# Hybrid attention and state-space block on one core: when the attention's sums, the gates' products and the gated unit's tanh are issued

## The chip, the core and the metric

The kernel runs on one core of a Trainium2 chip. The time is device microseconds of one execution. The kernel before took 1146.03 us in the median of three runs (1145.88 to 1149.12). The engines are TensorE (PE: matmuls; PEld: its weight loads), VectorE (DVE), ScalarE (ACT), GpSimd (POOL) and SyncE (SP, which issues most transfers). Each engine works through its own queue in the order in which the program issues; an instruction that waits holds up everything behind it on its engine.

## The reference

One decoder block on 512 tokens and 16 meta tokens, 1024 wide: a half-weighted SwiGLU unit, then a mixer, then a second half-weighted SwiGLU unit, with a norm ahead of each and one at the end. The mixer runs sliding-window attention and a state-space layer side by side and merges them through two sigmoid gates:

```
hn = rmsnorm(h, mix_norm)
q, k, v, u, g_attn, g_ssm = split(hn @ w_in)
attn = sliding_window_attention(q, k, v, sinks)     # 16 heads, 4 key heads, window 128, 16 meta keys, one sink per head
y = gelu(s5_ssm(u))
ssm = (y @ glu_a) * sigmoid(y @ glu_b)
merged = sigmoid(g_attn) * attn + sigmoid(g_ssm) * ssm
h = h + merged @ w_out
```

Everything is float32. The kernel keeps that precision by splitting each operand of a product into a high and a low part (`hi`, `lo`) and summing three matmuls (hi·hi, hi·lo, lo·hi) for one.

## The kernel before

**Units.** The work of TensorE is a row of units. A unit holds 128 output rows: its weights arrive by SyncE's transfers as raw float32, are split ahead of time by `prep_piece` (ScalarE copies the high part, line 173; VectorE subtracts to get the low part `wlo`, line 174), and are then used by 24 matmuls of 512 columns (line 238). Other work that TensorE must do is issued between these matmuls: `accumulate` (line 223) takes a list of callbacks and calls them at even distances. In the mixer that list has eleven places, cut 0 to cut 10.

**The mixer's thirty units** (loop from line 1304) are, by `MIX`, two each of: queries q1 (units 0, 1), state gates gs0 (2, 3), gated units glu0 (4, 5), q2 (6, 7), attention gates ga0 (8, 9), gs1 (10, 11), glu1 (12, 13), q3 (14, 15), ga1 (16, 17), gs2 (18, 19), glu2 (20, 21), ga2 (22, 23), gs3 (24, 25), ga3 (26, 27) and glu3 (28, 29). A unit's evacuation is put off into the next unit: `flush` at cut 0 of the next.

**The attention's sixteen blocks** (4 key heads times 4 blocks of 128 queries) run inside these units. Block n begins in unit `BEGIN[n]` and takes three units:

- in the first, `s1` for four heads at cuts 2, 4, 7 and 7: two score matmuls (1167, 1168) into one of two score buffers in PSUM, a masking reduction on VectorE (1170) that frees the score buffer, the exponential on ScalarE (1172); after the fourth head the denominator: `es` (1175, 1176), `den` (1177, 1178), and the probabilities normalised on VectorE (`pm`, the meta keys, 1181) and GpSimd (`E`, 1183);
- in the second, `s2o` and `s2p` at cut 7 transpose the probabilities (1191) and split them into `ph` and `pl` (1194, 1195); `s2m` at cut 8 does it for the meta keys (`ms`, 1212 and 1213), and GpSimd spreads them into `m4` (1215; the profile's name is m);
- in the third, `s3` at cut 5 multiplies by the values (1226) into `pv`, `s3m` at cut 7 adds the meta keys' product (1234), and `s3e` at cut 9 brings the sum out. The values are stored as high and low halves side by side, so `pv` has two halves of 64 partitions, and the sum of the two is the attention's output: ScalarE copies the lower half to `tb` (1240), and VectorE adds the halves into `AT` in two instructions (1242).

The PSUM pool of `pv` has one buffer (line 1078), that of the scores two (1076). `tb`, `ta`, `tg` and `tq` share a tag with four buffers (line 1091).

**The gates.** `ev_ga` multiplies an attention gate's output by the norm's factor (1257), takes the tanh (1258), multiplies into `AT` (1259) and, for rows below 6, adds the state-space part (`merge`, 1250). `unit_glu` makes two products of half the depth, `b` and then `a`, each with its own PSUM tile; its evacuation takes the tanh of `b` (1283), multiplies by `a` (1284) and by the state gate (1285). The weights for a later unit are prepared at cut 8. The order within a cut is that in which the loop's body calls `at_cut`.

Of the kernel before, what the change touches and what calls it, by code (L numbers as in the profile page):

```python
# [10 lines left out]
AF = mybir.ActivationFunctionType  # L11
ALU = mybir.AluOpType
# [25 lines left out]
PREPS = (6, 34)  # L38
KS1 = 8
VS = (1, 0, 2, 10, 13, 13)  # L40
CUT = {"s3": 5, "s3m": 7, "s3e": 9, "s1": (2, 4, 7, 7), "s2o": 7, "s2p": 7, "s2m": 8, "prep": 8, "ev": 0, "ks": 10, "vs": 7}
BEGIN = (1, 2, 3, 4, 6, 7, 10, 11, 13, 14, 15, 18, 19, 20, 21, 24)

NG = 32
# [21 lines left out]
def hybrid_block_kernel(  # L66
# [30 lines left out]
    V, S, G, PE, SY = nc.vector, nc.scalar, nc.gpsimd, nc.tensor, nc.sync  # L97
# [13 lines left out]
    def real(t):  # L111
        return t.rearrange("p (h c) -> p h c", h=2)[:, :, :256]
# [118 lines left out]
    def mm3(outs, hi, lo, rhi, rlo, nk, mids, k0=0):  # L231
        seq = []
        for k in range(nk):
            seq += [(hi, rhi, k), (hi, rlo, k), (lo, rhi, k)]

        def emit(w, r, k, start, stop):
            for o, sl in outs:
                PE.matmul(out=o, lhsT=w[:, k0 + k, :], rhs=sl(r, k), start=start, stop=stop)  # L238

        accumulate(seq, emit, mids)  # L240
# [10 lines left out]
    def mm512(ps, hi, lo, rhi, rlo, nk, mids, k0=0, packed=True):  # L251
        if packed:
            mm3([(ps, lambda r, k: r[:, k, :])], hi, lo, rhi, rlo, nk, mids, k0)
        else:
            mm3([(ps, lambda r, k: real(r[:, k, :]))], hi, lo, rhi, rlo, nk, mids, k0)
# [575 lines left out]
    def norm_hook(t_p, h, hgn, n, cols=COLS):  # L831
        def hook(d):
            split_hg(hgn, h, n, d, 0, cols)
            t = t_p.tile([128, cols], F32, tag="t1", name="sqd")
            S.activation(out=t, in_=h[:, d, :], func=AF.Square)
            if d == 0:
                G.tensor_copy(sqs[:, :cols], t)
            else:
                G.tensor_tensor(out=sqs[:, :cols], in0=sqs[:, :cols], in1=t, op=ALU.add)
        return hook  # L840
# [5 lines left out]
    units, _ = ffn_units(hg, hT, True, mm_ps, g_p, t_p, CHUNKS1, norm_hook(t_p, hT, hg2, 1), first_mm)  # L846
# [181 lines left out]
    def h2(t):  # L1028
        return t.rearrange("p (h c) -> p h c", h=2)
# [55 lines left out]
    AT = a_p.tile([128, ND, SEQ], F32, name="AT")  # L1085
# [4 lines left out]
    def tmp(name):  # L1090
        return a_p.tile([128, 512], F32, tag="t", name=name, bufs=4)
# [62 lines left out]

    att = {}

    def s1(n, h):
        k, b = divmod(n, 4)
        W = 144 if b == 0 else 272
        c0 = (0, 0, 144, 272)[b]  # L1160
        if h == 0:
            att[n] = [a_p.tile([128, 4, 272], F32, tag="E", name="E", bufs=2)]
            att[n] += [a_p.tile([128, 4], F32, tag=t, name=t, bufs=2) for t in ("mn", "den", "es")]
        E, mn, den, es = att[n][:4]
        q = Q[2 * k + h // 2][:, h % 2, 128 * b:128 * b + 128]
        ps = sc_ps.tile([128, 512], F32, tag="sc", name="ps_s")
        PE.matmul(out=ps[:, 0:W], lhsT=q, rhs=KH[:, k, c0:c0 + W], start=True, stop=False)  # L1167
        PE.matmul(out=ps[:, 0:W], lhsT=q, rhs=KL[:, k, c0:c0 + W], start=False, stop=True)  # L1168
        mk = mC[:, 128:272] if b == 0 else (mC if b == 2 else mA)
        V.tensor_tensor_reduce(out=E[:, h, 0:W], in0=ps[:, 0:W], in1=mk, scale=1.0,  # L1170
                               scalar=sinkn[:, 4 * k + h:4 * k + h + 1], op0=ALU.add, op1=ALU.min, accum_out=mn[:, h:h + 1])
        S.activation(out=E[:, h, 0:W], in_=E[:, h, 0:W], func=AF.Exp, scale=-1.0, bias=mn[:, h:h + 1], accum_out=den[:, h:h + 1])  # L1172
        if h != 3:
            return
        V.tensor_tensor(out=es, in0=mn, in1=sinkn[:, 4 * k:4 * k + 4], op=ALU.subtract)
        S.activation(out=es, in_=es, func=AF.Exp)
        V.tensor_tensor(out=den, in0=den, in1=es, op=ALU.add)
        V.reciprocal(out=den, in_=den)
        m0 = 128 if b == 2 else 0
        pm = a_p.tile([128, 4, 16], F32, tag="pm", name="pm", bufs=2)  # L1180
        V.tensor_tensor(out=pm, in0=E[:, :, m0:m0 + 16], in1=den.unsqueeze(2).to_broadcast([128, 4, 16]), op=ALU.mult)
        for c, w in (((0, 128), (144, 128)) if b == 2 else ((16, W - 16),)):
            G.tensor_tensor(out=E[:, :, c:c + w], in0=E[:, :, c:c + w], in1=den.unsqueeze(2).to_broadcast([128, 4, w]), op=ALU.mult)
        att[n] = (E, pm, [])
# [45 lines left out]
    pvs = {}  # L1230

    def s3m(n):
        pv, ms = pvs[n]
        PE.matmul(out=pv, lhsT=VM[:, n // 4, :], rhs=ms.rearrange("p h c -> p (h c)"), start=False, stop=True)

    def s3e(n):
        k, b = divmod(n, 4)
        pv, _ = pvs.pop(n)
        tb = tmp("tb")
        S.activation(out=tb[0:64], in_=pv[64:128, :], func=AF.Copy)  # L1240
        for e in range(2):
            V.tensor_tensor(  # L1242
                out=AT[64 * e:64 * e + 64, 2 * k:2 * k + 2, 128 * b:128 * b + 128],
                in0=pv[0:64].rearrange("p (i e c) -> p e i c", e=2, c=128)[:, e],
                in1=tb[0:64].rearrange("p (i e c) -> p e i c", e=2, c=128)[:, e], op=ALU.add)
# [3 lines left out]
    def merge(m):  # L1249
        V.scalar_tensor_tensor(out=AT[:, m, :], in0=gst.pop(m), scalar=0.5, in1=AT[:, m, :], op0=ALU.mult, op1=ALU.add)  # L1250
        if m >= 6:
            msplit(m)

    def ev_ga(m):
        def f(p):
            t = tmp("ta")
            V.tensor_tensor(out=h2(t), in0=p, in1=r512, op=ALU.mult)
            S.activation(out=t, in_=t, func=AF.Tanh, scale=0.5)
            V.scalar_tensor_tensor(out=AT[:, m, :], in0=t, scalar=1.0, in1=AT[:, m, :], op0=ALU.add, op1=ALU.mult)
            if m < 6:  # L1260
                merge(m)
        return f

    def ev_gs(m):
# [7 lines left out]
    def unit_glu(m):  # L1272
        cell = {}

        def mm(hi, lo, mids):
            n = (len(mids) + 1) // 2
            for key, k0, ms in (("b", 4, mids[:n]), ("a", 0, mids[n:])):
                cell[key] = mm_ps.tile([128, 512], F32, tag="mm", name="p")
                mm512(cell[key], hi, lo, YH, YL, 4, ms, k0)

        def ev():
            t = tmp("tg")
            S.activation(out=t, in_=cell["b"], func=AF.Tanh, scale=0.5)
            V.scalar_tensor_tensor(out=t, in0=t, scalar=1.0, in1=cell["a"], op0=ALU.add, op1=ALU.mult)
            V.scalar_tensor_tensor(out=gst[m], in0=gst[m], scalar=1.0, in1=t, op0=ALU.add, op1=ALU.mult)
            if m >= 6:
                merge(m)
        return mm, ev
# [3 lines left out]
    def msplit(m):  # L1292
        S.activation(out=mg[0][:, m, :], in_=AT[:, m, :], func=AF.Copy)
        V.tensor_tensor(out=mg[1][:, m, :], in0=AT[:, m, :], in1=fr(mg[0][:, m, :]), op=ALU.subtract)
# [8 lines left out]
    begin = dict(zip(BEGIN, range(16)))  # L1303
    for i, u in enumerate(units):
        cuts = [[] for _ in range(NCUT)]

        def at_cut(c, f, *a):
            cuts[c].append(lambda: f(*a))

        if i - 2 in begin:  # L1310
            for f, c in ((s3, "s3"), (s3m, "s3m"), (s3e, "s3e")):
                at_cut(CUT[c], f, begin[i - 2])
        if i in begin:
            for h in range(4):
                at_cut(CUT["s1"][h], s1, begin[i], h)
        if i - 1 in begin:
            for f, c in ((s2o, "s2o"), (s2p, "s2p"), (s2m, "s2m")):
                at_cut(CUT[c], f, begin[i - 1])
        at_cut(CUT["ev"], flush)
        if i == KS1:  # L1320
            at_cut(CUT["ks"], ksplit, 1)
            at_cut(CUT["ks"], vmeta, 1)
        for v, iv in enumerate(VS):
            if i == iv:
                at_cut(CUT["vs"], vsplit, *divmod(v, 3))
        at_cut(CUT["prep"], prep_piece)
        if i == len(units) - 2:
            mg += new_hg(SEQ)
            for m in range(6):
                at_cut(m, msplit, m)  # L1330

        step(*u, mids=[lambda fs=fs: [f() for f in fs] for fs in cuts], prep=False, hold=i < len(units) - 1)
# [59 lines left out]
    n = CHUNKS2[-1]  # L1392
# [60 lines left out]
    for j in range(2 * ND):  # L1453
        h, d = divmod(j, ND)
# [48 lines left out]
```

## Time and profile before

| what | value |
|---|---|
| median of three runs | 1146.03 us |
| the profiled execution, its own time | 1148.62 us |
| its span, first to last instruction | 1146.8 us |
| TensorE busy | 1127.8 us, 98% of the span |
| VectorE, ScalarE, GpSimd busy | 636.5, 410.4, 357.1 us |
| the mixer's thirty units | about 498 to 728 us of the span |
| mean granted TensorE clock | 0.990 |

Times in the rows are microseconds from the span's start, then the duration, the engine, the line, the operation, what it writes and reads with its shapes, how many were merged into the row, and in brackets the engine's idle time ahead of it and what ended it. A row of a group gives busy time and the mean of one in ns, a row of waits the engine and line that waited, for whom, the microseconds in total, how often, and the longest. A row of a stretch gives, for each engine, its busy time and its number of instructions, then the granted clock, the share of the transfer engines and GB/s.

### The profile page before, as it was taken

The page shows a single profiled execution, that of the slowest core. Times are in us where ns is not written, and L with a number is a line of the kernel's source. Part 1 is how long each engine was busy: PE and PEld are TensorE (multiplying, and loading weights), DVE is VectorE, ACT ScalarE, POOL GpSimd, SP SyncE. Part 2 cuts the span into 40 slices and gives each one's busy share as a digit, 9 for nine tenths or more (in the row PEclk, how much of TensorE's full clock was granted, in tenths as well). Part 3 has the DMA queues.
Part 4 walks back from the last instruction along what each step waited for, and adds up shares of the span by engine and source line. Part 5 has one row for each costly group of instructions (what it writes and reads, how often), then busy time and mean ns, then how long its engine had stood idle before and what let it go on. Part 6 is the DMA issues. An engine that isn't in the chain of part 4 may idle for free.

```text
span 1146.8 us, 17241 instructions
## 1 busy us (share of the span) xinstructions
PE 1127.8 (98%) x7006; PEld 1006.2 (88%) x7006; DVE 636.5 (55%) x960; ACT 410.4 (36%) x727; POOL 357.1 (31%) x488
## 2 busy tenths in 40 slices
PE   9999999999999999999999999999999999999997
PEld 7999999999999999977778778888888888888887
DVE  5446663655444464867767776664544444444454
ACT  5322232232222242465646554443322321322234
POOL 1966663542883030444444231020000000000003
PEclk7999999999999999999999999999999999999999
DMA  5423233232423246212211222432423224313222
GB/s 164 115 94 110 74 94 112 75 85 84 112 87 95 77 160 170 56 63 74 74 58 53 74 74 81 144 106 74 129 92 111 74 83 127 111 65 128 75 74 74
DMA packets 105583, 108.43 MB, mean 95 GB/s; under 512 B 7504, under 2 KB 101968, under 8 KB 105376
## 3 DMA queue, kind: packets, MB, share of 16 engines
q1 hardware_dynamic: 103104, 100.74, 28.0%
q0 software_dynamic: 2352, 6.52, 2.2%
q8 instruction: 55, 0.90, 0.3%
q14 instruction: 24, 0.20, 0.1%
q10 hardware_dynamic: 48, 0.07, 0.0%
HBM read 100.80 MB, written 5.34 MB: 93 GB/s over the span
## 4 chain that ended last, share of the span: by engine, by line
PE 88%; DVE 5%; ACT 4%; issue 2%; DMA 1%; POOL 0%; SPq 0%; DVEq 0%; POOLq 0%; ACTq 0%
PE p L238 59%; PE p L412 11%; PE p L414 9%; PE p L800 2%; PE pv L1226 1%; PE p L1398 1%; DVE wlo L174 1%; ACT whi L173 1%; PE ps_t L1191 1%; DVE AT L1242 1%; PE ps_s L1167 1%; ACT E L1172 1%; PE ps_s L1168 1%; DMA xb<-in_x_dram 1%; ACT qs L1144 0%
## 5 line engine op out<-in xcount | busy, mean ns | idle before, releaser
L238 PE MATMUL p<-hgh,whi 128*128 128x264 f32 (+1 forms) x1408 | 403.6, 333 | 0.1
L238 PE MATMUL p<-hgl,whi 128*128 128x264 f32 (+1 forms) x1408 | 403.1, 332 | 0.0
L238 PE MATMUL p<-hgh,wlo 128*128 128x264 f32 (+1 forms) x1408 | 401.2, 331 | 0.0
L174 DVE TENSOR_TENSOR wlo<-raw,whi 128x1024 fp32r<-128x1024 f32 (+2 forms) x192 | 257.7, 1342 | 91.6 <-ACT whi L173 89.4
L238 PEld LDWEIGHTS p<-hgh,whi 128*128 128x128 f32 x1408 | 238.9, 188 | 26.0 <-issue 0.8
L238 PEld LDWEIGHTS p<-hgh,wlo 128*128 128x128 f32 x1408 | 238.6, 189 | 23.5
L238 PEld LDWEIGHTS p<-hgl,whi 128*128 128x128 f32 x1408 | 238.9, 188 | 22.4
L173 ACT ACTIVATE whi<-raw 128x1024 fp32r<-128x1024 f32 (+2 forms) x192 | 187.5, 979 | 133.5 <-PE p L414 72.2
L1414 POOL TENSOR_TENSOR acc<-acc,zq 128x256 f32<-128x256 f32 x12 | 8.9, 738 | 349.8 <-ACT zq L1407 349.7
L432 DVE SCALAR_TENSOR_TENSOR hT<-p,hT 128x528 f32<-128x528 f32 (+1 forms) x56 | 39.1, 698 | 87.1 <-PE p L414 52.2
L384 ACT ACTIVATE t<-t 128x528 f32<-128x528 f32 (+1 forms) x44 | 28.1, 639 | 165.0 <-DVE t L383 164.9
L394 ACT ACTIVATE gh<-t 128x528 fp32r<-128x528 f32 (+1 forms) x44 | 28.1, 639 | 160.6 <-DVE t L393 160.6
L412 PE MATMUL p<-gh,whi 128*128 128x264 f32 x352 | 72.6, 288 | 0.7 <-DVE hT L432 0.5
L412 PE MATMUL p<-gl,whi 128*128 128x264 f32 x352 | 71.5, 284 | 0.0
L412 PE MATMUL p<-gh,wlo 128*128 128x264 f32 x352 | 71.4, 284 | 0.0
L383 DVE TENSOR_TENSOR t<-p,r_bc 128x528 f32<-128x528 f32 (+1 forms) x44 | 30.7, 698 | 71.3 <-PE p L238 68.1
L393 DVE TENSOR_TENSOR t<-p,t 128x528 f32<-128x528 f32 (+1 forms) x44 | 30.7, 698 | 65.4 <-PE p L238 65.0
L412 PEld LDWEIGHTS p<-gh,whi 128*128 128x128 f32 x352 | 54.5, 189 | 1.9 <-issue 0.8
L414 PE MATMUL p<-gh,whi 128*128 128x512 f32 x144 | 56.0, 389 | 0.0
L414 PE MATMUL p<-gl,whi 128*128 128x512 f32 x144 | 56.0, 389 | 0.0
L414 PE MATMUL p<-gh,wlo 128*128 128x512 f32 x144 | 56.0, 389 | 0.0
L385 DVE TENSOR_TENSOR t<-t,r_bc 128x528 f32<-128x528 f32 (+1 forms) x44 | 37.2, 846 | 32.4 <-ACT t L384 32.4
(322 smaller groups left out, 1502.2 us busy)
## 6 DMA issues: line engine op xcount, KB each, us to landing
raw<-in_ffn_w_dram SPq DMA_DIRECT2D x42, 1024.0 KB, 5.4
raw<-in_ffn_w_dram SPq DMA_DIRECT2D x24, 768.0 KB, 4.3
raw<-in_w_in_dram SPq DMA_DIRECT2D x16, 1024.0 KB, 5.5
raw<-in_ffn_w_dram SPq DMA_DIRECT2D x12, 512.0 KB, 3.6
raw<-in_w_out_dram SPq DMA_DIRECT2D x4, 1024.0 KB, 8.1
h_keep<-hT POOLq DMA_DIRECT2D x1, 2112.0 KB, 7.3
raw<-in_ssm_glu_a_dram SPq DMA_DIRECT2D x4, 512.0 KB, 3.6
raw<-in_ssm_glu_b_dram SPq DMA_DIRECT2D x4, 512.0 KB, 5.3
```

What stands on the lines that cost most here:

```text
L173: S.activation(out=hi, in_=src, func=AF.Copy)
L174: V.tensor_tensor(out=lo, in0=src, in1=fr(hi), op=ALU.subtract)
L238: PE.matmul(out=o, lhsT=w[:, k0 + k, :], rhs=sl(r, k), start=start, stop=stop)
L383: V.tensor_tensor(out=t1, in0=cell[1], in1=rb(), op=ALU.mult)
L384: S.activation(out=t1, in_=t1, func=AF.Silu)
L385: V.tensor_tensor(out=t1, in0=t1, in1=rb(), op=ALU.mult)
L393: V.tensor_tensor(out=t3, in0=cell[3], in1=cell["t1"], op=ALU.mult)
L394: S.activation(out=gh, in_=t3, func=AF.Copy)
L412: PE.matmul(out=p[:, h, :HALF], lhsT=wt[:, k, :], rhs=gs[k][c][:, h, :], start=start, stop=stop)
L414: PE.matmul(out=p, lhsT=wt[:, k, :], rhs=gs[k][c].rearrange("p h c -> p (h c)"), start=start, stop=stop)
L432: V.scalar_tensor_tensor(out=hv(hT, d), in0=cell["p"], scalar=0.5, in1=hv(hT, d), op0=ALU.mult, op1=ALU.add)
L800: PE.matmul(out=p[:, h, :HALF], lhsT=w[:, k, :], rhs=r[:, k, h * HALF:(h + 1) * HALF], start=(n == 0), stop=(n == 3 * ND - 1))
```

## The change

Three things move; no instruction is added or taken away.

1. `tb` is now issued by `s3m`, right behind the meta keys' product at cut 7, and no longer by `s3e`. The two additions of `s3e` move from cut 9 to cut 7 in units where no new block begins. In the seven units in which the third unit of one block is the first of another (3, 4, 6, 13, 15, 20, 21) they are issued inside that other block's `s1`, after `es` and ahead of `den` (the call `fill`).
2. The second half of an attention gate's evacuation (1259 and the merge) is put into a list of its own, which is emptied at cut 6 of the same unit; the first half stays at cut 0.
3. The tanh of `b` in `unit_glu` is issued right behind `b`'s matmuls, ahead of those of `a`, in the unit itself.

```diff
-CUT = {"s3": 5, "s3m": 7, "s3e": 9, "s1": (2, 4, 7, 7), ..., "prep": 8, "ev": 0, "ks": 10, "vs": 7}
+CUT = {"s3": 5, "s3m": 7, "s3e": 7, "ev2": 6, "s1": (2, 4, 7, 7), ..., "prep": 8, "ev": 0, "ks": 10, "vs": 7}
...
-    def s1(n, h):
+    def s1(n, h, fill):
...
         S.activation(out=es, in_=es, func=AF.Exp)
+        if fill:
+            fill()
         V.tensor_tensor(out=den, in0=den, in1=es, op=ALU.add)
...
     def s3m(n):
         pv, ms = pvs[n]
         PE.matmul(out=pv, lhsT=VM[:, n // 4, :], rhs=ms.rearrange("p h c -> p (h c)"), start=False, stop=True)
+        tb = tmp("tb")
+        S.activation(out=tb[0:64], in_=pv[64:128, :], func=AF.Copy)
+        pvs[n] = (pv, tb)
 
     def s3e(n):
         k, b = divmod(n, 4)
-        pv, _ = pvs.pop(n)
-        tb = tmp("tb")
-        S.activation(out=tb[0:64], in_=pv[64:128, :], func=AF.Copy)
+        pv, tb = pvs.pop(n)
...
+    pend2 = []
+
+    def flush2():
+        while pend2:
+            pend2.pop(0)()
+
     def ev_ga(m):
         def f(p):
             t = tmp("ta")
             V.tensor_tensor(out=h2(t), in0=p, in1=r512, op=ALU.mult)
             S.activation(out=t, in_=t, func=AF.Tanh, scale=0.5)
-            V.scalar_tensor_tensor(out=AT[:, m, :], in0=t, scalar=1.0, in1=AT[:, m, :], op0=ALU.add, op1=ALU.mult)
-            if m < 6:
-                merge(m)
+
+            def second():
+                V.scalar_tensor_tensor(out=AT[:, m, :], in0=t, scalar=1.0, in1=AT[:, m, :], op0=ALU.add, op1=ALU.mult)
+                if m < 6:
+                    merge(m)
+            pend2.append(second)
         return f
...
                 mm512(cell[key], hi, lo, YH, YL, 4, ms, k0)
+                if key == "b":
+                    t = cell["t"] = tmp("tg")
+                    S.activation(out=t, in_=cell["b"], func=AF.Tanh, scale=0.5)
 
         def ev():
-            t = tmp("tg")
-            S.activation(out=t, in_=cell["b"], func=AF.Tanh, scale=0.5)
+            t = cell["t"]
...
-            for f, c in ((s3, "s3"), (s3m, "s3m"), (s3e, "s3e")):
-                at_cut(CUT[c], f, begin[i - 2])
+            at_cut(CUT["s3"], s3, begin[i - 2])
+            at_cut(CUT["s3m"], s3m, begin[i - 2])
+            fill = lambda n=begin[i - 2]: s3e(n)
+            if i not in begin:
+                at_cut(CUT["s3e"], fill)
+        else:
+            fill = None
         if i in begin:
             for h in range(4):
-                at_cut(CUT["s1"][h], s1, begin[i], h)
+                at_cut(CUT["s1"][h], s1, begin[i], h, fill)
...
         at_cut(CUT["ev"], flush)
+        at_cut(CUT["ev2"], flush2)
```

More of the change, by code (lines that the diff above doesn't have):

```diff
@@ L40 @@
 VS = (1, 0, 2, 10, 13, 13)
-CUT = {"s3": 5, "s3m": 7, "s3e": 9, "s1": (2, 4, 7, 7), "s2o": 7, "s2p": 7, "s2m": 8, "prep": 8, "ev": 0, "ks": 10, "vs": 7}
+CUT = {"s3": 5, "s3m": 7, "s3e": 7, "ev2": 6, "s1": (2, 4, 7, 7), "s2o": 7, "s2p": 7, "s2m": 8, "prep": 8, "ev": 0, "ks": 10, "vs": 7}
 BEGIN = (1, 2, 3, 4, 6, 7, 10, 11, 13, 14, 15, 18, 19, 20, 21, 24)
```

## The prediction

> **What bounds the kernel now.** I read the page first, then the stretch in which the changed code runs, then TensorE's waits in that stretch, and last the queues of VectorE, ScalarE and GpSimd around each wait.
>
> ```profile
> span 1146.8 us, 17241 instructions
> PE 1127.8 (98%) x7006; PEld 1006.2 (88%) x7006; DVE 636.5 (55%) x960; ACT 410.4 (36%) x727; POOL 357.1 (31%) x488
> PE 88%; DVE 5%; ACT 4%; issue 2%; DMA 1%; POOL 0%; SPq 0%; DVEq 0%; POOLq 0%; ACTq 0%
> ...
> 498.00:735.00 237.00, 228.30 (x1098) 184.74 (x1096) 172.31 (x377) 130.28 (x302) 88.24 (x59) 0.99 0.24 75
> 735.00:838.00 103.00, 103.00 (x460) 85.44 (x460) 51.60 (x63) 36.93 (x49) 12.07 (x9) 1.00 0.32 102
> ```
>
> TensorE is the bound: busy for 98% of the span and 88% of the chain. It has idle time where the mixer's thirty units run (498 to 735 us, columns PE, PEld, DVE, ACT, POOL): 237.00 − 228.30 = 8.7 us, while the next 103 us have none. So the change is worth at most those waits and what hangs on them. TensorE's waits between 496 and 735 us:
>
> ```profile
> PE ps_s L1167 <- DVE mn L1170: 4.5, 4, 2.0
> PE pv L1226 <- DVE AT L1242: 4.1, 8, 0.9
> ```
>
> ```profile
> 671.46 0.39 PE L238 MATMUL p<-YH,wlo 128*128 128x512 f32 x1
> 671.69 0.40 PE L238 MATMUL p<-YH,whi 128*128 128x512 f32 x1
> 671.93 0.39 PE L1234 MATMUL pv<-m,VM 128*128 128x512 f32 x1
> ...
> 670.00 0.47 PE L1226 MATMUL pv<-ph,VB 128*128 128x512 f32 x1 [0.78 <-DVE AT L1242]
> ...
> 687.11 0.47 PE L1226 MATMUL pv<-ph,VB 128*128 128x512 f32 x1 [0.18 <-DVE AT L1242]
> ```
>
> A matmul's record lasts 0.39 us, but undisturbed starts are 0.23 us apart (671.69 − 671.46). So a wait costs its idle time plus 0.39 − 0.23 = 0.16 us of lost overlap. The eight pv waits cost 4.1 + 8 × 0.16 = **5.4 us**. The pool for pv has one buffer, so the next block's value products cannot start before the sum of L1242 has read the last one.
>
> **Part 1: the sum (s3m, s3e).** Unit 20, a unit whose softmax will take the sum in, shows why it comes late; ScalarE's, TensorE's and GpSimd's rows stand with VectorE's:
>
> ```profile
> 664.74 0.16 DVE L1175 TENSOR_TENSOR es<-mn,sinkn 128x4 f32<-128x4 f32 x1
> 665.56 0.16 DVE L1177 TENSOR_TENSOR den<-den,es 128x4 f32<-128x4 f32 x1 [0.67 <-ACT es L1176]
> ...
> 666.12 0.68 DVE L1195 TENSOR_TENSOR pl<-ps_t,ph 128x512 fp32r<-128x512 f32 x1
> 666.83 0.28 DVE L1213 TENSOR_TENSOR ms<-ps_tm,ms 64x128 fp32r<-64x128 f32 x1
> 667.16 1.93 DVE L174 TENSOR_TENSOR wlo<-raw,whi 128x1024 fp32r<-128x1024 f32 x1
> 669.01 0.84 DVE L1242 TENSOR_TENSOR AT<-pv,tb 64x256 f32<-64x256 f32 x2
> ...
> 663.09 0.39 PE L1234 MATMUL pv<-m,VM 128*128 128x512 f32 x1
> ...
> 664.32 0.52 ACT L1172 ACTIVATE E<-E,mn 128x272 f32<-128x272 f32 x1 [1.95 <-DVE mn L1170]
> ...
> 667.15 0.60 ACT L1240 ACTIVATE tb<-pv 64x512 f32<-64x512 f32 x1
> ...
> 667.97 2.02 POOL L1215 TENSOR_TENSOR m<-ms,hm 128x512 fp32r<-128x512 f32 x1
> ```
>
> The value products are complete at 663.09 + 0.39 = 663.5. The copy tb waits until 667.15 behind the weights' copy, and the sum until 669.01 behind pl, ms and wlo. After the change tb is issued at cut 7: it can run from 663.5 to 664.1, in ScalarE's idle stretch before the exponential at 664.32. The two additions (0.84 us) follow es and run from 664.90 to 665.74, where VectorE waited 0.67 us for ScalarE anyway. Visible price: 0.84 − 0.67 = 0.17 us of VectorE. pv is free at 665.8 instead of 669.9, and TensorE would come for it at 670.00 − (0.78 + 0.16) = 669.1: 3 us to spare. Five of the eight waits follow such filled units (3, 4, 15, 20, 21). The other three follow units without a softmax (8, 16, 22), where the sum comes right after s3m:
>
> ```profile
> 634.82 1.29 DVE L1195 TENSOR_TENSOR pl<-ps_t,ph 128x512 fp32r<-128x512 f32 x2 [2.89 <-ACT ph L1194]
> ...
> 636.58 2.11 DVE L174 TENSOR_TENSOR wlo<-raw,whi 128x1024 fp32r<-128x1024 f32 x1 [0.15 <-ACT whi L173]
> 638.61 0.84 DVE L1242 TENSOR_TENSOR AT<-pv,tb 64x256 f32<-64x256 f32 x2
> ```
>
> There VectorE was idle for 2.89 us ahead of pl; the additions fit in, and even if pl slips by the whole 0.84 us, the sum ends about 3 us earlier. I take all 5.4 us as gained; bounds 2.7 (half come back under another name) and 5.4. No instruction is added and no DMA moves in this part.
>
> What queues behind tb: the exponentials, ph, ms and the weights' copy on ScalarE, at most 0.60 us later, and through ms GpSimd's m, which s3m needs. **m is late next.** In block 12 it ends at 667.97 + 2.02 = 669.99 and s3m starts at 671.93; without the wait of 0.94 us that is 671.0. The slack of 1.0 us covers 0.17 us, and also 0.60 us. If that cover were gone, each us of lateness of m would be a us on TensorE.
>
> **Part 2: the gates' second half.** The worst single wait is in unit 10, where a gate of unit 9 is evacuated (VectorE's queue, TensorE's two matmuls around the wait, and two stretches with the granted clock third from the right):
>
> ```profile
> 577.79 2.38 DVE L174 TENSOR_TENSOR wlo<-raw,whi 128x1024 fp32r<-128x1024 f32 x1
> 580.09 0.84 DVE L1242 TENSOR_TENSOR AT<-pv,tb 64x256 f32<-64x256 f32 x2
> 580.96 0.69 DVE L1257 TENSOR_TENSOR ta<-p,r_bc 128x512 f32<-128x512 f32 x1
> 582.41 0.69 DVE L1259 SCALAR_TENSOR_TENSOR AT<-ta,AT 128x512 f32<-128x512 f32 x1 [0.76 <-ACT ta L1258]
> 583.14 0.69 DVE L1250 SCALAR_TENSOR_TENSOR AT<-ts,AT 128x512 f32<-128x512 f32 x1
> 583.75 0.49 DVE L1170 CUSTOM_DVE_ANT_0 E<-ps_s,mC,sinkn 128x272 f32<-128x272 f32 x1
> ...
> 581.87 0.40 PE L238 MATMUL p<-hgh,whi 128*128 128x512 f32 x1
> 584.30 0.39 PE L1167 MATMUL ps_s<-KH,qs 128*128 128x272 f32 x1 [2.04 <-DVE mn L1170]
> ...
> 581.00:584.30 3.30, 1.26 (x6) 0.69 (x4) 2.51 (x6) 0.65 (x2) 0.00 (x0) 1.00 0.87 272
> 585.20:588.60 3.40, 3.40 (x11) 2.73 (x10) 2.26 (x10) 2.74 (x9) 1.41 (x2) 0.51 0.00 0
> ```
>
> The third score needs a score buffer, so the first reduction (L1170, ready to end at 584.2). In front of it stand the idle 0.76 and the two products of the gate, 1.4 us; together 2.2 us (583.75 − 580.96 − 0.69 = 2.1). At cut 6 they come behind the first two reductions, so TensorE can go on at 584.30 − 2.1 = 582.2. It would come at 581.87 + 0.23 = 582.1, or earlier by unit 9's pv wait, one of the eight (5.4 / 8 = 0.7 at the mean). So of 2.04 + 0.16 = 2.2 us, 0.1 to 0.8 stays. I take 0.5, the middle: **1.7 us** gained; bounds 0 (the reductions stay as late) and 2.2. The price, 1.4 us ahead of the third reduction in units 10, 18 and 24, is VectorE's; in unit 10 the normalised scores still reach GpSimd no later than the 587.19 of before, since the block's VectorE work is the same in sum, and their transposes follow only in the next unit, at 593.44:
>
> ```profile
> 587.19 3.02 POOL L1183 TENSOR_TENSOR E<-E,den 128x512 f32<-128x512 f32 x2 [6.87 <-DVE den L1178]
> ...
> 593.44 0.82 PE L1191 MATMUL ps_t<-ident,E 128*128 128x128 f32 x6
> ```
>
> **The clock.** Right behind that gap the granted clock is 0.51 for 3.40 us: 3.40 × 0.49 = **1.6 us** lost; the mixer's mean of 0.99 leaves room for one such stretch. I tie it to the gap, since TensorE was busy for 1.26 of the 3.30 us before. The Trainium skill, TensorE: Matmul & The Clock Gate, Part 1, lets the half rate come after an idle window of about 3.4 us; the idle stretch here was 2.04 us, so by the rule as it stands the 1.6 us would not hang on this gap, and the sum would be 1.6 us smaller. This trace shows the drop after a partly idle window.
>
> **Part 3: the tanh of the gated unit.** It ran at the head of the next unit, behind the weights' copy and tb, and VectorE's first product of the gate waited behind the sum. It moves to the middle of its own unit, where ScalarE waits for the reductions (1.95 us idle at 664.32); nothing is added, and the first product then waits for TensorE alone. It shows on TensorE in one place:
>
> ```profile
> 616.42 0.39 PE L1167 MATMUL ps_s<-KH,qs 128*128 128x272 f32 x1 [0.19 <-DVE mn L1170]
> 510.43 0.31 PE L1167 MATMUL ps_s<-KH,qs 128*128 128x144 f32 x1 [1.54 <-DVE mn L1170]
> 518.20 0.39 PE L1167 MATMUL ps_s<-KH,qs 128*128 128x272 f32 x1 [0.76 <-DVE mn L1170]
> ```
>
> Unit 14's wait (616.42): with the sum and its tanh earlier, 0.19 + 0.16 = **0.3 us** gained; bounds 0 and 0.35. The waits at 510.43 and 518.20 (2.6 us with their overlap) belong to blocks 0 and 1, before any sum or gate: they stay.
>
> **Costs.** New small waits for m or a reduction, which no row shows: between 0 and the 2.7 us that I allowed to come back; I take 0.5, nearer to zero, since the slack just worked out is longer than every delay.
>
> **Sum.** 5.4 + 1.7 + 1.6 + 0.3 − 0.5 = 8.5 us. The profiled execution took 1148.62 us (span 1146.8 and 1.8 around it): 1140.1. The median of the runs is 1146.03, 2.6 us below it, and one run of the three (1149.12) is as long as the profiled one. One or two half-clock windows of 1.6 us would explain that, so the median may not hold the clock term: I carry half of it, 7.7 us, to the median: **1138.3 us**.
>
> **Rivals.**
> (a) *Only the pv waits go*: unit 10's reductions stay behind wlo (2.38 us there against 1.93 in unit 20) or the clock step comes regardless. 5.4 + 0.3 − 0.5 = 5.2: 1140.8. For it: wlo and the additions alone hold VectorE until 580.93. Against: the gate's 2.1 us are plainly in front. The rule of the Trainium skill cited above would take this side.
> (b) *The wait changes its name*: VectorE, busy for 172.31 of 237.00 us, is the second bound; TensorE stops at reductions or m instead. Half of 5.4 and the 0.3 remain: 3.0, 1143.0. Against it: 64.7 us of VectorE are idle.
> (c) *Slower*: the softmax chain becomes the path. In the seven filled units (3, 4, 6, 13, 15, 20, 21) tb (0.60) and the additions (0.84) all land ahead of den: 7 × 1.44 = 10.1; in units 10, 18 and 24 the gate's 1.4 us ahead of the third reduction: 4.2. Minus the 5.4 of the pv waits and the 3.3 of unit 10 with its clock: +5.6, 1151.6. It decides once m or the normalised scores come over 1 us later than now; the idle 0.67 us at den and ScalarE's 1.95 us speak against it.
> (d) *It doesn't do what it says*: tb, ta, tg and tq share four buffers, and a tb issued earlier may wait for a tq that GpSimd still reads; nothing moves: 1146.0.
>
> **How the numbers follow.** Forecast 58%, (a) 22%, (b) 13%, (c) 4%, (d) 3%. A measurement of this kernel tells some 0.3% (3.4 us) from no change: faster, below 1142.6, is the forecast and (a), 80%; within it (b) and (d), 16%; slower 4%. The range goes from all waits of the list gone with the full clock term (5.4 + 2.2 + 1.6 + 0.35 = 9.6, 1136.4, less 0.9 for a run without other drops) to (b): 1135.5 to 1143.0. That holds the forecast, (a) and half of (b), and the rest stays out.
>
> **What would show it.** Right: no TensorE wait of pv on AT; the additions between es and den in filled units; in unit 10 the first two reductions ahead of L1259; granted clock 1.00 there; mixer's idle time near 4 us. Wrong: TensorE waiting for m (L1215), for normalised scores, or for reductions behind a gate's second half; tb waiting for GpSimd; the mixer still 237 us long.

## The result, and the profile after

The changed kernel took **1138.71 us** in the median of four runs (1135.81 to 1139.63); the kernel before, run beside it, took 1147.53 us in the median of four. The ratio is **0.9919**, with a 95% interval from 0.9892 to 0.9946, so 8.8 us are gone. The same kernel, run again later, gave 1136.57 us (1136.03 to 1138.31, five runs) against 1148.16 us, a ratio of 0.9902 (0.9885 to 0.9918). The profiled execution's own time is 1139.31 us, against 1148.62 us before. Of all the runs below, one stands apart: 1376.01 us at a granted clock of 0.749, in the kernel with `m` written twice; that kernel's ratio leaves it out.

Three views answer to those of before: the page's head, the stretch of the thirty units (columns as there: length, then PE, PEld, DVE, ACT, POOL, granted clock, transfers), and TensorE's waits in it and in the unit behind it (496 to 735 us, as before). The kernel after:

```profile
span 1137.5 us, 17229 instructions
PE 1124.6 (99%) x7006; PEld 1005.8 (88%) x7006; DVE 631.9 (56%) x960; ACT 410.0 (36%) x727; POOL 360.4 (32%) x488
```

```profile
499.30:717.60 218.30, 215.88 (x1062) 177.74 (x1061) 163.23 (x371) 127.29 (x300) 89.62 (x57) 1.00 0.23 73
```

```profile
PE ps_s L1167 <- DVE mn L1170: 2.3, 2, 1.5
PE p L238 <- DVE hgl L1308: 0.2, 1, 0.2
```

The thirty units of the kernel before, cut at their own ends, for comparison:

```profile
498.40:727.60 229.20, 220.50 (x1062) 178.18 (x1061) 167.02 (x372) 128.35 (x300) 86.34 (x57) 0.99 0.22 69
```

The mixer is 10.9 us shorter. TensorE's idle time in it falls from 229.20 − 220.50 = 8.7 us to 218.30 − 215.88 = 2.4 us. The other 4.6 us are busy time that shrank: 1.6 us of the half-clock stretch, ten times 0.16 us of the overlap that the eight waits and those of units 10 and 14 had cost, and smaller steps that are told with the sum below. All eight waits of the value products are off the list. The two waits of `ps_s` that stay are those of blocks 0 and 1; the one for `hgl` is new and lies in the first output unit. The trace has 12 instructions fewer than before; all 12 are semaphore instructions, which count as no engine's work.

The whole divides into four stages. Each starts with the first 512-column matmul of unit 0, of the first output unit behind the mixer, and of the second; the last ends with the span (us, from the profiled executions):

| stage | before | after | difference |
|---|---|---|---|
| up to unit 0 | 498.43 | 499.34 | +0.9 |
| the thirty units | 229.14 | 218.23 | −10.9 |
| first output unit | 5.44 | 6.10 | +0.66 |
| the rest | 413.84 | 413.86 | 0.0 |

The stage ahead of unit 0 holds no changed instruction; what its 0.9 us are is told in the last section.

**The filled unit.** Unit 20 of the kernel after, VectorE's queue and then ScalarE's copy (start, duration, and in brackets the idle time ahead):

```profile
656.65 0.16 DVE L1175 TENSOR_TENSOR es<-mn,sinkn 128x4 f32<-128x4 f32 x1
656.73 0.84 DVE L1245 TENSOR_TENSOR AT<-pv,tb 64x256 f32<-64x256 f32 x2
657.60 0.16 DVE L1179 TENSOR_TENSOR den<-den,es 128x4 f32<-128x4 f32 x1
...
659.21 1.92 DVE L174 TENSOR_TENSOR wlo<-raw,whi 128x1024 fp32r<-128x1024 f32 x1
...
655.43 0.59 ACT L1238 ACTIVATE tb<-pv 64x512 f32<-64x512 f32 x1 [0.54 <-PE pv L1236]
```

The copy waits for the meta keys' product alone, and the additions run between `es` and `den`, where before VectorE stood idle for 0.67 us. They end at 657.57; the next value products start at 660.96, 3.4 us later.

**Unit 10.** VectorE's queue of the kernel after, then TensorE's third score there:

```profile
576.51 1.51 DVE L174 TENSOR_TENSOR wlo<-raw,whi 128x1024 fp32r<-128x1024 f32 x1
577.93 0.68 DVE L1266 TENSOR_TENSOR ta<-p,r_bc 128x512 f32<-128x512 f32 x1
578.54 0.49 DVE L1170 CUSTOM_DVE_ANT_0 E<-ps_s,mC,sinkn 128x272 f32<-128x272 f32 x1
...
579.37 0.76 DVE L1270 SCALAR_TENSOR_TENSOR AT<-ta,AT 128x512 f32<-128x512 f32 x1
580.17 0.69 DVE L1253 SCALAR_TENSOR_TENSOR AT<-ts,AT 128x512 f32<-128x512 f32 x1
...
579.97 0.29 PE L1167 MATMUL ps_s<-KH,qs 128*128 128x272 f32 x1
```

The first reduction starts 0.61 us after `ta`, not 2.79 us after it as before (583.75 − 580.96), and the score has no wait. Two more things differ. The sum no longer stands between the low part of the weights and `ta`, and that low part took 1.51 us where it took 2.38. The second goes with GpSimd's rows: before, its product `KL` (L1119) ran from 577.38 to 579.08 us when the low part began at 577.79; after, its product (L1118) ran from 575.22 to 576.93 when the low part began at 576.51. Behind GpSimd's end the low part took 1.09 us in both. So where VectorE's subtraction falls in GpSimd's work sets how long it takes here; no run varied that alone.

### The profile page after: what moved, and what is told of

Read it like the earlier page. It is cut to its first block, busy times and chain, and to the rows that moved or that the text cites. A ratio compares the mean times of both kernels' runs of the same rounds, so it can differ in the third digit from the quotient of the medians.

```text
span 1137.5 us, 17229 instructions
## 1 busy us (share of the span) xinstructions
PE 1124.6 (99%) x7006; PEld 1005.8 (88%) x7006; DVE 631.9 (56%) x960; ACT 410.0 (36%) x727; POOL 360.4 (32%) x488
## 4 chain that ended last, share of the span: by engine, by line
PE 90%; DVE 4%; ACT 3%; issue 1%; DMA 1%; POOL 0%; DVEq 0%; POOLq 0%; SPq 0%; ACTq 0%
PE p L238 61%; PE p L412 11%; PE p L414 9%; PE p L800 2%; PE p L1418 1%; PE pv L1228 1%; PE ps_t L1193 1%; DVE wlo L174 1%; ACT whi L173 1%; PE ps_x L746 1%; PE ps_s L1167 1%; PE ps_s L1168 1%; DMA xb<-in_x_dram 0%; DVE hgl L1308 0%; PE pv L1236 0%
## 5 line engine op out<-in xcount | busy, mean ns | idle before, releaser
L174 DVE TENSOR_TENSOR wlo<-raw,whi 128x1024 fp32r<-128x1024 f32 (+2 forms) x192 | 253.2, 1319 | 89.2 <-ACT whi L173 86.7
```

What stands on the lines that cost most here:

```text
L174: V.tensor_tensor(out=lo, in0=src, in1=fr(hi), op=ALU.subtract)
```

## The experiments

All stand against the kernel before on the same chip, whose median was 1147.96 us (19 runs) for the first four, 1148.16 us (18 runs) for the next four, and 1148.10 us (9 runs) for the last two. "Mixer" is the length of the thirty units in the profiled execution, as in the table above.

### Part 1 alone

The hunks of `s1`, `s3m`, `s3e` and the loop; the gate's second half follows its first at once, and the tanh of `b` stays where it was.

```diff
 (against the kernel after)
-            pend2.append(second)
+            second()
...
-                if key == "b":
-                    t = cell["t"] = tmp("tg")
-                    S.activation(out=t, in_=cell["b"], func=AF.Tanh, scale=0.5)
...
-            t = cell["t"]
+            t = tmp("tg")
+            S.activation(out=t, in_=cell["b"], func=AF.Tanh, scale=0.5)
```

> Part 1 alone (copy at cut 7, additions at cut 7 or inside the softmax); the gate's second half and the gated unit's tanh stay where they were. Theory (the eight pv waits come from the additions' place in VectorE's queue): no wait of pv on the additions is left, 5.4 us less, and unit 10's wait of 2 to 2.7 us for the reductions stays, so about 1142 us against 1147.5 before; a half-clock stretch behind that gap again if the gap makes it. Rival (the parts help only together, VectorE being the bound): half of the pv waits come back as waits for reductions or for m, 1145 us or more.

Measured: 1137.36 us (1136.88 to 1138.48), ratio 0.9914 (0.9896 to 0.9931); mixer 220.31 us, 8.8 less than before. That is less than the 1142 us expected. All eight waits are gone; unit 10's is still there, but shorter than expected. VectorE's queue and TensorE's score in this kernel, and the two stretches around it:

```profile
572.91 1.50 DVE L174 TENSOR_TENSOR wlo<-raw,whi 128x1024 fp32r<-128x1024 f32 x1
574.34 0.68 DVE L1266 TENSOR_TENSOR ta<-p,r_bc 128x512 f32<-128x512 f32 x1
575.77 0.76 DVE L1270 SCALAR_TENSOR_TENSOR AT<-ta,AT 128x512 f32<-128x512 f32 x1 [0.76 <-ACT ta L1267]
...
577.73 0.39 PE L1167 MATMUL ps_s<-KH,qs 128*128 128x272 f32 x1 [1.20 <-DVE mn L1170]
```

```profile
575.28:578.69 3.41, 2.21 (x13) 1.52 (x11) 2.70 (x7) 1.44 (x5) 0.64 (x2) 1.00 0.89 283
578.69:582.10 3.41, 3.41 (x17) 2.79 (x16) 2.27 (x10) 2.68 (x9) 1.48 (x2) 1.00 0.07 24
```

The gate's two products (the second starts at 576.57) still stand ahead of the reductions, but TensorE waits 1.20 us there instead of 2.04 (1.36 us instead of 2.20 from start to start), and no half-clock stretch follows. Part 1 thus gains more than its eight waits: 0.84 us of unit 10, the clock step behind it, and unit 14's 0.36 us as well. In time it cannot be told from the whole change.

### Part 2 alone

```diff
 (against the kernel before)
-            V.scalar_tensor_tensor(out=AT[:, m, :], in0=t, scalar=1.0, in1=AT[:, m, :], op0=ALU.add, op1=ALU.mult)
-            if m < 6:
-                merge(m)
+
+            def second():
+                V.scalar_tensor_tensor(out=AT[:, m, :], in0=t, scalar=1.0, in1=AT[:, m, :], op0=ALU.add, op1=ALU.mult)
+                if m < 6:
+                    merge(m)
+            pend2.append(second)
...
+        at_cut(6, flush2)
```

> Part 2 alone (the attention gate's second product and the merge at cut 6). Theory: unit 10's wait of 2.2 us is gone or below 0.5 us, the half-clock stretch behind it with it (1.6 us), the eight pv waits stay within 1 us of 5.4 in sum: about 3.5 us less, 1144 us. Rival (the clock step does not hang on the gap): the half-clock stretch is there though the gap is gone, 2 us less, 1145.5. Rival (the products only move the delay to the third and fourth reduction): TensorE waits there and nothing is gained.

Measured: 1146.41 us (1142.58 to 1147.50, ten runs), ratio 0.9982 (0.9970 to 0.9995); mixer 225.79 us, 3.35 less. TensorE's waits in this kernel:

```profile
PE pv L1226 <- DVE AT L1242: 4.1, 8, 0.9
PE ps_s L1167 <- DVE mn L1170: 2.5, 3, 1.5
```

The eight waits stand as before to the tenth. Unit 10's is gone, and no stretch has a lower clock, although the low part of the weights took 2.38 us here as in the kernel before. So it was enough to take the gate's products out of the way to end that wait, and the clock step went with it. The 3.35 us are the 1.7 + 1.6 of the prediction, reached otherwise: 2.2 of the wait, about 1.5 of the clock, less 0.3 in small ones. The median moved by 1.6 us only; what a median holds beside the mixer is told in the last section.

### Part 3 alone

```diff
 (against the kernel before)
                 mm512(cell[key], hi, lo, YH, YL, 4, ms, k0)
+                if key == "b":
+                    t = cell["t"] = tmp("tg")
+                    S.activation(out=t, in_=cell["b"], func=AF.Tanh, scale=0.5)
...
-            t = tmp("tg")
-            S.activation(out=t, in_=cell["b"], func=AF.Tanh, scale=0.5)
+            t = cell["t"]
```

> Part 3 alone (tanh of the gated unit right behind its first product). Theory: unit 14's wait of 0.35 us goes, and a new wait of some 0.5 us appears in the first output unit, since the tanh now stands ahead of the weights' copy in the last gated unit and pushes the low weights ahead of that unit's own gate: no change beyond 0.5 us, 1147 to 1148 us. Rival (the tanh frees VectorE's queue, and the pv waits behind gated units shrink): 1 to 2 us less.

Measured: 1149.58 us (1145.80 to 1150.61, ten runs), ratio 1.0013 (1.0001 to 1.0026); mixer 229.17 us, the same as before. The waits in this kernel, and unit 14's:

```profile
PE ps_s L1167 <- DVE mn L1170: 4.6, 4, 2.1
PE pv L1226 <- DVE AT L1242: 4.3, 8, 0.9
PE p L238 <- DVE hgl L1296: 0.2, 1, 0.2
```

```profile
616.83 0.39 PE L1167 MATMUL ps_s<-KH,qs 128*128 128x272 f32 x1 [0.20 <-DVE mn L1170]
```

Unit 14 waits as before, so the 0.3 us that the prediction gave to the tanh do not come from it. A new wait shows in the first output unit instead, which takes 6.06 us where it took 5.44.

### The sum behind the softmax's vector work

```diff
 (against the kernel after: in s1)
-        if fill:
-            fill()
         V.tensor_tensor(out=den, in0=den, in1=es, op=ALU.add)
...
+        if fill:
+            fill()
```

> The changed kernel, but in the seven filled units the additions are issued behind the whole softmax (behind the normalisation) and no longer between es and den. Theory (what matters is that they stand ahead of pl, ms and the low weights; the hidden 0.67 us at den is not on the path): no pv wait, within 0.5 us of the changed kernel, 1138.7 us. Rival (the place inside the softmax is what brings the gain, because VectorE has no slack): pv waits or waits for reductions of 2 us and more come back, 1141 us or more.

Measured: 1137.97 us (1136.72 to 1140.09), ratio 0.9919 (0.9899 to 0.9940); mixer 219.16 us, 0.93 more than after. No value product waits. In this kernel, GpSimd's `m` of block 13 and the meta keys' product that needs it:

```profile
666.46 2.08 POOL L1217 TENSOR_TENSOR m<-ms,hm 128x512 fp32r<-128x512 f32 x1 [0.52 <-DVE ms L1215]
...
668.05 0.39 PE L238 MATMUL p<-hgh,whi 128*128 128x512 f32 x1
668.59 0.50 PE L1236 MATMUL pv<-m,VM 128*128 128x512 f32 x1
```

From 668.05 to 668.59 TensorE loses 0.54 − 0.23 = 0.31 us to `m`, which ends at 668.54. So the gain of part 1 comes from being ahead of `pl`, `ms` and the low weights; the slot between `es` and `den` is worth another 0.9 us of mixer, which the timed runs cannot tell.

### GpSimd's m written twice

```diff
 (against the kernel after)
-        G.tensor_tensor(out=m4, ...)
+        for _ in range(2):
+            G.tensor_tensor(out=m4, ...)
```

> The changed kernel, with GpSimd's spreading of the meta keys' probabilities (m, 1.04 to 2.02 us) issued twice into the same tile, so that m is about 1.04 us later in each of the 16 blocks; the result is the same. Theory (m is what is late next): in the changed kernel m ends 0.42, 0.12, 0.92, 0.59, 0.79 and 0.35 us ahead of the product that needs it in blocks 0, 4, 8, 9, 12 and 13, over 1.04 us in the others; so TensorE waits for m in those six blocks, 0.62 + 0.92 + 0.12 + 0.45 + 0.25 + 0.69 = 3.1 us in sum, and the thirty units take about 221 us instead of 218.2. Rival (m has slack everywhere, as in the kernel before, where it cost 0.23 us once): under 0.5 us.

Measured: 1142.33 us in the median of five runs (1141.58 to 1143.43 but for the run named at the head), ratio 0.9949 (0.9932 to 0.9967); mixer 223.50 us, 5.3 more than after. The new wait in this kernel:

```profile
PE pv L1237 <- POOL m L1218: 3.4, 6, 0.9
```

From start to start, seven blocks (0, 2, 4, 8, 9, 12, 13) lose 4.6 us to it, none of which shows in the kernel after; 3.1 us in six blocks were expected. `m` is next in line, in more blocks than the one the prediction looked at.

### The copy early, the additions late

```diff
 (against the kernel before)
     def s3m(n):
...
+        tb = tmp("tb")
+        S.activation(out=tb[0:64], in_=pv[64:128, :], func=AF.Copy)
+        pvs[n] = (pv, tb)
...
     def s3e(n):
-        pv, _ = pvs.pop(n)
-        tb = tmp("tb")
-        S.activation(out=tb[0:64], in_=pv[64:128, :], func=AF.Copy)
+        pv, tb = pvs.pop(n)
```

> The kernel before with the copy of pv's lower half at cut 7 alone; the two additions stay at cut 9, gates and tanh as before. Theory (the additions' place in VectorE's queue, behind pl, ms and the low weights, is what is late, not the copy): the eight pv waits stay within 0.7 us of 5.4 in sum, the thirty units take 229 us as before, 1147 to 1148 us. Rival (the copy, queued behind the weights' copy on ScalarE, is what is late): the waits shrink to under half, 1144.5 or less.

Measured: 1149.64 us (1145.50 to 1152.96, ten runs), ratio 1.0013 (0.9998 to 1.0028); mixer 230.69 us, 1.5 more than before. The waits in this kernel:

```profile
PE ps_s L1167 <- DVE mn L1170: 6.0, 6, 1.8
PE pv L1226 <- DVE AT L1243: 4.1, 5, 0.9
```

From start to start the eight waits cost 5.1 us, where they cost 5.4. Ahead of none of them had VectorE waited for the copy, in the kernel before or in this one: the additions follow the low weights at once. So the copy was not what came last, and the additions' place in VectorE's queue sets when `pv` comes free.

The sum hides two shifts. The five waits behind filled units stay or grow, while those in units 9, 17 and 23 go or fall to 0.1 us, because the low weights ahead of their additions took 1.23 us instead of 2.10. In the kernel before, GpSimd's `m` started 0.01 to 0.03 us ahead of each of these low weights and took 1.04 us; here it starts 0.02 to 0.05 us behind them and takes 2.08 to 2.10. In these rows, the one that starts first takes its own time and the other waits it out. The mixer's 1.5 us more come mostly from two new waits for reductions, of 0.98 us each, in units 18 and 24. In unit 17 ScalarE now idles 1.38 us until the product that `tb` needs is done, the weights' copy behind `tb` comes at 643.09 instead of 640.75, and VectorE, idle for 1.51 us until then, brings the low weights, the gate and the reductions late; unit 23 is alike.

### Parts 1 and 2 with the weights' work of units 0 and 1 put off

This was meant to remove the two waits that are left, by taking the low parts of the weights out of blocks 0 and 1.

```diff
 (against the kernel after, without part 3)
-        at_cut(CUT["prep"], prep_piece)
+        if i in (1, 2):
+            at_cut(5, prep_piece)
+        if i > 1:
+            at_cut(CUT["prep"], prep_piece)
```

> Parts 1 and 2 without part 3, and the weights' preparation of units 0 and 1 put off to cut 5 of the next unit, behind the first two reductions. Theory: the two waits left (1.7 and 0.9 us, blocks 0 and 1) go or fall below 0.5 us each, the wait of 0.5 us in the first output unit goes: thirty units in about 216 us instead of 218.2, 1136 us. Rival (the weights of unit 2 or 3 then come late): a wait of TensorE for the weights of 1 us or more takes their place, 1138 to 1139 us.

Measured: 1140.39 us (1137.95 to 1140.98), ratio 0.9933 (0.9917 to 0.9949); mixer 219.79 us, 1.6 more than after. The waits in this kernel:

```profile
PE ps_tm L1212 <- DVE mn L1170: 2.5, 1, 2.5
PE p L238 <- DVE wlo L174: 0.8, 1, 0.8
PE ps_s L1167 <- POOL qs L1145: 0.7, 1, 0.7
```

Here the waits did change their name: the weights come too late for their own unit, and the reductions behind them too late for the next transposes.

### The kernel after once more

> The changed kernel once more, beside the others on the same chip. Theory (the scatter between executions lies in the half-clock start, not in the mixer): thirty units in 218.2 us within 0.3 us again, whatever the whole execution takes; the unit ahead of them starts between 495.5 and 499.6 us. Rival (the mixer scatters itself): its thirty units differ by over 1 us.

Measured: the 1136.57 us given at the head; mixer 218.21 us, against 218.23 in the first profile. Unit 0 starts at 496.20 us, 3.1 us earlier than there. The mixer repeats to 0.02 us; what varies lies ahead of it.

### Parts 1 and 2, the tanh where it was

```diff
 (against the kernel after)
-                if key == "b":
-                    t = cell["t"] = tmp("tg")
-                    S.activation(out=t, in_=cell["b"], func=AF.Tanh, scale=0.5)
...
-            t = cell["t"]
+            t = tmp("tg")
+            S.activation(out=t, in_=cell["b"], func=AF.Tanh, scale=0.5)
```

> Parts 1 and 2, without part 3. Theory (part 3 gives nothing that part 1 does not give, and costs the wait of 0.5 us in the first output unit): thirty units in 218.2 us within 0.3 us, the first output unit in 5.6 us or less instead of 6.1, 0.5 us less in all, which the timed runs cannot tell. Rival (part 3 does its work in units 14 and 22): thirty units take over 218.6 us.

Measured: 1138.86 us (1138.39 to 1139.39), ratio 0.9924 (0.9910 to 0.9938); mixer 218.23 us, the same as after. The only wait left on the list of this kernel is that of blocks 0 and 1, and the first output unit takes 5.62 us, not 6.10. What the tanh does there: in the kernel after, around the end of unit 29 (VectorE, then TensorE)

```profile
718.38 1.23 DVE L174 TENSOR_TENSOR wlo<-raw,whi 128x1024 fp32r<-128x1024 f32 x1 [0.74 <-ACT whi L173]
...
722.36 0.69 DVE L1308 TENSOR_TENSOR hgl<-AT,hgh 128x512 fp32r<-128x512 f32 x1 [0.70 <-ACT hgh L1307]
...
723.11 0.50 PE L238 MATMUL p<-hgl,whi 128*128 128x512 f32 x1 [0.23 <-DVE hgl L1308]
```

and in this kernel

```profile
717.82 1.23 DVE L174 TENSOR_TENSOR wlo<-raw,whi 128x1024 fp32r<-128x1024 f32 x1 [0.26 <-ACT whi L173]
...
721.80 0.69 DVE L1306 TENSOR_TENSOR hgl<-AT,hgh 128x512 fp32r<-128x512 f32 x1 [0.70 <-ACT hgh L1305]
```

With the tanh early, ScalarE's copy of the next weights comes behind it, VectorE idles 0.74 us for that copy instead of 0.26, and everything down to `hgl`, for which the output unit waits, comes about 0.5 us later. Part 3 costs half a microsecond on TensorE and gains none; the timed runs cannot tell it from nothing.

### Five gaps in TensorE's work

Additions on VectorE into a tile that nobody reads, between 4 and 7 of them ahead of the first reduction of blocks 6, 9, 11, 13 and 15, hold TensorE at five places.

```diff
 (against the kernel after: in s1)
+        if h == 0:
+            for _ in range({6: 5, 9: 4, 11: 7, 13: 7, 15: 7}.get(n, 0)):
+                V.tensor_tensor(out=scr, in0=AT[:, 0, :], in1=AT[:, 1, :], op=ALU.add)
```

> The changed kernel with idle work on VectorE (additions into a tile that nobody reads: 5, 4, 7, 7 and 7 of some 0.62 us) ahead of the first reduction of blocks 6, 9, 11, 13 and 15, so that TensorE idles some 2.1 to 2.5 us in units 10, 15, 18, 20 and 24; the result is the same. Theory (the clock is judged by aligned stretches of 3.41 us, as the starts of the recorded clock steps show, and a stretch that is busy for less than about 45% is followed by one of half clock): a half-clock stretch of 3.4 us follows those gaps that lie inside one aligned stretch, some but not all of the five; a gap astride two of them, with each busy over half, has none. Rival 1 (any gap of 2 us or more makes it): five of five. Rival 2 (the step in unit 10 of the kernel before had another cause, such as what the other engines did there; an idle time under 3.4 us never makes it): none of five.

Measured in a single run: 1162.53 us; mixer 241.25 us, 23.0 more than after. Two of the five stretches of this kernel that hold a gap, each with the stretch behind it:

```profile
581.00:584.41 3.41, 1.03 (x7) 0.91 (x8) 3.31 (x9) 1.05 (x4) 0.00 (x0) 1.00 0.56 199
584.42:587.83 3.41, 3.41 (x11) 2.63 (x10) 2.56 (x10) 2.34 (x8) 0.50 (x1) 0.50 0.00 0
649.27:652.68 3.41, 0.63 (x4) 0.33 (x3) 3.31 (x9) 0.47 (x2) 0.00 (x0) 1.00 0.48 169
652.68:656.09 3.41, 3.41 (x10) 2.83 (x10) 2.61 (x10) 2.36 (x10) 0.00 (x0) 0.50 0.00 0
```

After each of the five the clock is 0.50 for one stretch of 3.41 us, though no gap is 3.4 us long. I had expected some of the five and not all: five of five is what the first rival said. The gaps came out longer than planned (2.46 to 3.21 us lost), and so this run does not tell a rule by the gap's length from one by its place. Two other kernels do, in the last section.

## Why the prediction was right, step by step

- **The pv waits, 5.4 us: right.** From start to start the eight steps shrank by 5.4 us. All eight went in every kernel with part 1, and none went in part 2 or part 3 alone. The cause was as told: not the copy (the early copy alone left the sum of the idle times at 4.1 us) but the two additions behind `pl`, `ms` and the low weights.
- **Unit 10, "I take 0.5, the middle", to stay: mis-sized.** Nothing stayed; the whole 2.2 us went. And the step credited it to part 2 alone. Part 1 alone took 0.84 us of it: with the sum out of the queue, and the low part of the weights at 1.50 us instead of 2.38, `ta` came sooner. The two parts overlap here, in these 0.84 us and in the clock step, which either part removes, so their gains alone do not add: 8.8 + 3.35 = 12.2 us against 10.9 together.
- **The clock, 1.6 us, tied to the gap: right in mechanism.** The step stands behind every long gap of unit 10 (before, part 3 alone, the copy alone) and behind none of the shortened ones. By the Trainium skill, TensorE: Matmul & The Clock Gate, Part 1, an idle window of about 3.4 us would have had to come first; here gaps of 1.8 to 2.1 us were enough. The size was a little off: 3.40 × 0.49 is 1.67 and not 1.6, and the steps of that stretch shrank by 1.6 us.
- **"I carry half of it … to the median": wrong reason.** All three profiles of kernels with the long gap had the step. What scatters between executions is, as far as the profiles show, the time ahead of unit 0. The medians moved by 8.8 us; the interval, 6.2 to 12.4 us, holds the whole sum of 8.5 and the 7.7 as well. The second measurement, 11.6 us (9.4 to 13.2), lies above both.
- **Part 3, 0.3 us and "nothing is added": failed.** The step named the sum and the tanh together. Unit 14's 0.36 us went in part 1 alone, where the sum no longer stands ahead of the reductions, and stayed with part 3 alone. Instead the tanh holds up the weights' copy in unit 29, and the output unit pays 0.5 us. The step looked for ScalarE's idle time in one unit and did not follow the copy behind the tanh through to the mixer's end.
- **The waits of blocks 0 and 1 stay: right**, at 1.5 and 0.8 us in every kernel but the one that moved the weights' work.
- **"m is late next", with 1.0 us of slack: right, and tighter than told.** The prediction looked at block 12. In the kernel after, GpSimd's `m` of blocks 4 and 13, each with the product that needs it:

```profile
563.73 2.02 POOL L1217 TENSOR_TENSOR m<-ms,hm 128x512 fp32r<-128x512 f32 x1
...
565.88 0.43 PE L1236 MATMUL pv<-m,VM 128*128 128x512 f32 x1
...
668.94 2.02 POOL L1217 TENSOR_TENSOR m<-ms,hm 128x512 fp32r<-128x512 f32 x1
...
671.30 0.39 PE L1236 MATMUL pv<-m,VM 128*128 128x512 f32 x1
```

  Block 4 has 0.1 us to spare, block 13 has 671.30 − 670.96 = 0.34 us, and block 12 (`m` from 660.00, product at 662.81) 0.8. In the kernel before, block 4 had 0.05 us, and TensorE had already lost 0.2 us to `m` there. Block 13's is why the sum behind the softmax costs TensorE 0.31 us.
- **Costs, 0.5 us: near the mark for other reasons.** A wait of 0.28 us for a reduction in unit 19 is part 2's (it stands in part 2 alone too, where before it was 0.16), and the first output unit grew by 0.66, 0.48 of it by part 3 and the rest by part 2 (5.62 us with part 2 alone). Of the new waits for `m` that the term named, none came.
- **The sum.** Seen in the mixer: 5.37 + 2.20 + 1.57 + 0.36, and m's 0.24 of block 4, less 0.12 in unit 19, make 9.6 of 10.9 us. Most of the other 1.3 us had no term: the value product behind each of the eight waits now starts 0.23 us after the one before it, not 0.31 (0.6 us together), and nine score steps of units 7, 10 and 14 fell from 0.17 to 0.23 us each to 0.12 or 0.13 (0.8 us, of which unit 21 gives back 0.3). The rest is spread over steps too small to name. Head and output unit take 1.6 back: 9.3 us in the profiled executions, against 8.5 forecast. The forecast for the median, 1138.3 us, lies 0.4 us from the 1138.71 measured, and that closeness is luck in part: the kernel before came out 1.5 us higher than the 1146.03 from which the forecast starts, and the gain 1.1 us larger than the 7.7 taken off. Rival (a) fell with the clock and unit 10, (b) with the empty list of waits, (c) with the medians and the idle slot at `den`, (d) with the copy that waited for TensorE alone.

## What to carry to other kernels

When one engine waits for a buffer, read who stands ahead of the instruction that frees it in that instruction's own queue: here 0.84 us of additions came some 4 us late behind work that nobody needed yet, and moving them cost TensorE nothing that the trace shows, because they fell into a wait of VectorE that was there already. Follow what is moved to the last unit as well as to the fullest, since early work on an in-order engine puts off all that is behind it, and try each part alone: two of the three parts cut into the same wait, and the third gave nothing.

## What the runs showed of the hardware that was not expected

**The clock goes by fixed stretches, not by the length of a gap.** The half-clock stretches lie on a fixed grid: the two shown for the kernel with five gaps start 652.68 − 584.42 = 68.26 us apart, 20 times 3.413 us. Cut at the borders of that grid (in a kernel without such a stretch, counted from the last clock step of its trace), every half-clock stretch of the mixer follows one in which TensorE was busy for under half. Two kernels tell length and place apart. In the kernel with the early copy, TensorE's wait in unit 10, and the stretch that holds it with the next:

```profile
585.04 0.39 PE L1167 MATMUL ps_s<-KH,qs 128*128 128x272 f32 x1 [1.79 <-DVE mn L1170]
```

```profile
583.25:586.66 3.41, 1.62 (x10) 1.41 (x10) 3.15 (x11) 1.64 (x6) 0.00 (x0) 1.00 0.72 249
586.66:590.07 3.41, 3.41 (x10) 2.66 (x9) 2.30 (x7) 2.02 (x7) 2.13 (x2) 0.50 0.00 0
```

In the kernel with the weights' work put off, a longer wait, which lies across the border of two stretches:

```profile
519.90 0.30 PE L1212 MATMUL ps_tm<-ident,pm 128*64 128x128 f32 x1 [2.47 <-DVE mn L1170]
```

```profile
515.69:519.10 3.41, 1.74 (x12) 1.27 (x11) 0.90 (x1) 2.45 (x6) 2.43 (x2) 1.00 0.00 0
519.11:522.52 3.41, 2.62 (x12) 2.19 (x13) 2.64 (x11) 2.64 (x9) 0.85 (x1) 1.00 0.51 150
```

A gap of 1.79 us inside one stretch (busy 1.62 / 3.41 = 0.48) was followed by half clock; a gap of 2.47 us shared between two (0.51 and 0.77) was not. Over all the profiles, the eight stretches of the mixer that are busy for 0.18 to 0.48 are each followed by half clock, and none of those busy for 0.51 or more is. How close to one half the border lies, and whether the same gap elsewhere in the stretch would always escape, was not tried further.

**The start's slow clock ends at different times.** Unit 0 starts between 495.75 and 499.69 us in twelve profiles, though the code ahead of it is the same. In the same early stretch of the kernel before, after, and with part 1 alone:

```profile
16.00:19.40 3.40, 3.40 (x15) 2.34 (x13) 1.33 (x4) 2.68 (x7) 0.00 (x0) 0.50 0.54 154
```

```profile
16.00:19.40 3.40, 3.40 (x14) 2.67 (x14) 1.43 (x4) 2.68 (x7) 0.00 (x0) 1.00 0.53 152
```

```profile
16.00:19.40 3.40, 3.40 (x25) 2.83 (x24) 2.65 (x8) 2.87 (x7) 0.00 (x0) 1.00 0.52 152
```

The kernel after has 14 matmuls there, as few as the 15 at a clock of 0.50 before, although its column shows 1.00; with part 1 alone it is 25. The spacing says the same: 264-column matmuls behind one another start 0.22 us apart there in the kernel after (16.20 and 16.42 us), and 0.12 to 0.13 us apart with part 1 alone (18.12 and 18.24 us). The count goes with the start of unit 0 in all twelve profiles: with 13 to 15 it starts at 498.43 to 499.69 us (seven profiles), with 20 at 496.53 and 496.77, with 25 at 495.75 to 496.20 (three). So the clock column misses the slow start in some of them, and up to 4 us of an execution's time go with how long the start takes. That is as much as part 2 is worth, and so one profiled execution against another does not show a part of that size; the length of the thirty units does.
